# A gather by fp32 products, an earlier second layer and 17 weight slots in two expert stages

## Chip, cores and metric

One core of a Trainium2 chip runs the whole program in one launch. The metric is the device time of that launch in microseconds (us); lower is better. Engines: PE (TensorE; matmuls, and PEld its weight loads), DVE (VectorE), ACT (ScalarE), POOL (GpSimd) and SP (SyncE, which here only issues DMAs). Each engine runs its own instructions in order.

## The reference, cut to what matters

Two blocks of layers on 512 tokens of width 1024. The first has two layers, and each ends in a mixture of experts. The change touches only these two mixtures:

```python
def _ec_moe(h, router, w1, w3, w2):        # 16 experts, each takes its top 64 of 512 tokens
    probs = softmax(h @ router, over the tokens)
    gates, idx = lax.top_k(probs, cap)     # cap = 64 tokens for each expert
    xs = h[bidx, idx]                      # gather
    a = xs @ w1[e]; g = xs @ w3[e]         # 1024 x 1024 each
    y = (silu(a) * g) @ w2[e] * gates      # 1024 x 1024
    return zeros.at[bidx, idx].add(y)      # scatter

x = x + g2 * _ec_moe(modulate(rmsnorm(x)), ...)
```

All is float32.

## The kernel before

`moe` (L1079) is one expert stage; it runs twice, for layers 0 and 1. Sixteen experts go as eight pairs q = 0 to 7; the two experts of a pair share PE, each with 64 of its 128 columns (tokens).

**Weights.** The three matrices of a pair come as 24 blocks of 1 MiB: 8 of w1, 8 of w3, 8 of w2, the two experts by turns. I number the blocks of a stage from 0 to 191; pair q has 24q to 24q + 23. `expert_load` (L949) issues one block on SP's queue, into the next slot of a fixed cycle, `EORDER` (L275): -1 is one of the four buffers of the ring pool, 0 to 9 are pools of one 8 KB (per partition) buffer each, opened one above the other for this stage (`more`, L1094), -2 is a buffer of the long-lived pool. There are 15 slots, so block b goes where block b - 15 lay and its DMA waits on SP until the last matmul that reads that block is done; the loads behind it in SP's queue wait with it. The first 15 are issued ahead of the stage, while PE still runs the projection of the mixer before (`pre`, L1100), each as soon as its memory is free.

**One pair.** `expert_mm` (L1157) takes the blocks in rounds of two, 16 PE instructions a round (each fp32 matmul is two instructions). w1 and w3 go into four PSUM banks `mm`. ACT and DVE make m = silu(w1) * w3 in the tile `em`; PE transposes it (L1263), DVE or ACT copies it back, and w2 (`expert_mm` again, into two `ac` banks) follows. `weigh` (L1265) multiplies by the gates and makes two parts of the result in `ey`, and `scatter` (L1271) adds it to x by products with a one-hot; that is done in the rounds 2 and 3 of the next pair's w1 (`rest`). `em` and `ey` share one buffer.

**The gather.** The token rows of pair 0 are gathered by fp32 products of x with a scaled one-hot (`pick_first`, L1132), between the first rounds of its w1. The other pairs go in groups (1), (2, 3), (4, 5), (6, 7): `gather` (L1103) makes the one-hot `oh` on DVE from the positions `pT` that `topk` finds, `pick` (L1119) gathers by products, `gates` (L1139) gathers the gate values. The products are made in two parts: `xn` is the normalized x as a rounded fp32r part (`xnh`) and the rest (`xnl`), `prp` the same of the probabilities; so a group has 8 column blocks x 4 token tiles x 2 parts = 64 products, of 128 columns for one pair and 256 for two. ACT makes xnh and DVE xnl (L1244, L1245). The gather for the next group stands behind the last w3 of a group and ahead of that pair's transposes and w2.

**What sets the order.** On PE the order is that of the code (`manual_schedule`, L1211). On DVE, ACT and POOL a scheduler places an instruction by what is ready; on SP the loads go in the order of the code.

Of the kernel before, what the change touches and what calls it, by code (L numbers as in the profile page):

```python
# [10 lines left out]
F32 = mybir.dt.float32  # L11
F32R = mybir.dt.float32r
BF16 = mybir.dt.bfloat16
AF = mybir.ActivationFunctionType
ALU = mybir.AluOpType
AX = mybir.AxisListType
PSUM = bass.MemoryType.PSUM

P = 128
D = 1024  # L20
# [5 lines left out]
NT = 4  # L26
# [243 lines left out]
class Builder:  # L270
    NBASE = 4
    X1, X2, X3, X4, X5, X6 = 2, 1, 3, 1, 7, 1
    NSTREAM, SDEPTH, SBUFS = 3, 2, 4
    EXTRA = 10
    EORDER = ((3, 2, 8, 9, 7, 0, 1, -1, -1, -1, -1, 4, 5, 6, -2), (-1, 7, 0, 6, 1, 8, 9, -1, -1, 5, -1, 2, 3, 4, -2))  # L275

    def __init__(self, ctx, tc, a, out):
        self.ctx, self.tc, self.nc, self.a, self.out = ctx, tc, tc.nc, a, out
# [800 lines left out]
    def moe(self, l, fin):  # L1079

        nc, a, tc, x = self.nc, self.a, self.tc, self.x
# [4 lines left out]
        pos = mp.tile([16, 512], BF16, name=f"pos{l}")  # L1086
        pT = mp.tile([P, NT, 16], F32, name=f"pT{l}")
        gts = mp.tile([P, 8], F32, name=f"gts{l}")

        xn = [self.pp.tile([P, NT, D], F32R, tag="hp0", name=f"xnh{l}"), mp.tile([P, NT, D], F32R, name=f"xnl{l}")]  # L1090
        prp = mp.tile([P, NT, 8, 2, 2], F32R, name=f"prp{l}")
        rt = self.pp.tile([P, KD // 2, 512], F32, tag="hp1", name=f"rt{l}")

        more = [es.enter_context(tc.tile_pool(name=f"r2{i}{l}", bufs=1, reuse_waits="tile")) for i in range(self.EXTRA)]  # L1094
# [8 lines left out]
        def gather(qs):  # L1103

            n = len(qs)
            oh = mp.tile([P, NT, 2, P], F32R, tag="oh", name=self.nm("oh"))
            o = oh[:, :, 0:n].rearrange("p t q (e s) -> p t (q e) s", e=2)
            nc.vector.tensor_tensor(o, self.iota[:, None, None, :].to_broadcast([P, NT, 2 * n, 64]),
                                    pT[:, :, 2 * qs[0]:2 * qs[0] + 2 * n, None].to_broadcast([P, NT, 2 * n, 64]), op=ALU.is_equal)
            xs = mp.tile([P, KD, 2, P], F32, tag="xsT", name=self.nm("xsT"))  # L1110
            return xs, oh
# [7 lines left out]
        def pick(qs, xs, oh):  # L1119
            w = len(qs) * P  # L1120
            for k0 in range(0, KD, 2):
                p = self.mm("ac" if k0 % 4 else "tr")
                for k in (k0, k0 + 1):
                    pk = p[:, (k - k0) * 256:(k - k0) * 256 + w]
                    for i in range(2):
                        for t in range(NT):
                            nc.tensor.matmul(pk, xn[i][:, t, k * P:(k + 1) * P], oh[:, t, 0:len(qs)].rearrange("p q s -> p (q s)"),  # L1127
                                             start=(i == t == 0), stop=(i == 1 and t == NT - 1))
                for k in (k0, k0 + 1):
                    modulate(k, xs[:, k, 0:len(qs)].rearrange("p q s -> p (q s)"), p[:, (k - k0) * 256:(k - k0) * 256 + w])  # L1130

# [7 lines left out]
        def gates(qs, oh):  # L1139

            p = self.mm("tr")
            v = p[:, 0:4 * len(qs)].rearrange("p (q u e) -> p q u e", u=2, e=2)
            for i, q in enumerate(qs):
                for t in range(NT):
                    if q:
                        nc.tensor.matmul(p[:, 4 * i:4 * i + 4], oh[:, t, i], prp[:, t, q].rearrange("p u e -> p (u e)"),
                                         start=(t == 0), stop=(t == NT - 1))
                    else:
                        nc.tensor.matmul(p[:, 0:2], oh0[:, 1, t], pr[:, t, 0:2], start=(t == 0), stop=(t == NT - 1))
            for e in range(2):  # L1150
                s = slice(64 * e, 64 * e + 64)
                if qs[0]:
                    nc.vector.tensor_reduce(gts[s, qs[0]:qs[0] + len(qs)], v[s, :, :, e], axis=AX.X, op=ALU.add)
                else:
                    nc.vector.tensor_copy(gts[s, 0:1], p[s, e:e + 1])

        def expert_mm(ps, lhs, before=None):  # L1157
            for i in range(4):
# [52 lines left out]
        with tc.manual_schedule(engines={mybir.EngineType.PE}):  # L1211
            for q in range(8):
# [20 lines left out]
                if q == 0:  # L1233
                    p = self.mm("tr")
                    sc = mp.tile([P, 512], F32R, tag="sc", name=self.nm("sc"))
                    for t in range(NT):
                        nc.tensor.transpose(p[:, t * P:(t + 1) * P], oh0[:, 1, t], self.ident)
                    nc.scalar.activation(out=sc, in_=p, func=AF.Copy)
                    gates((0,), None)
                    g2 = self.bcast_gate(mp, l, 1)  # L1240
                    with tc.issue_after(ohi.ins):
                        topk()
                    for t in range(NT):
                        nc.scalar.activation(out=xn[0][:, t], in_=x[:, t], func=AF.Copy, scale=rr[:, t:t + 1])  # L1244
                        nc.vector.scalar_tensor_tensor(xn[1][:, t], x[:, t], rr[:, t:t + 1], xn[0][:, t].bitcast(F32), op0=ALU.mult, op1=ALU.subtract)  # L1245
                    for t in range(NT):
                        v = pr[:, t].rearrange("p (q e) -> p q e", e=2)
                        nc.scalar.activation(out=prp[:, t, :, 0], in_=v, func=AF.Copy)
                        nc.vector.tensor_tensor(prp[:, t, :, 1], v, prp[:, t, :, 0].bitcast(F32), op=ALU.subtract)
                em = self.pp.tile([P, 2, D], F32, tag="hp1", name=self.nm("em"))  # L1250
                m, mT = em[:, 0], em[:, 1].rearrange("p (k s) -> p k s", k=KD)
                for j in range(2):
                    js = slice(j * 512, (j + 1) * 512)
                    nc.scalar.activation(out=m[:, js], in_=acc[0][j], func=AF.Silu)  # L1254
                    nc.vector.tensor_tensor(m[:, js], m[:, js], acc[1][j], op=ALU.mult)  # L1255
                if q == groups[g][-1] and q < 7:
                    xs, oh = gather(groups[g + 1])
                    pick(groups[g + 1], xs, oh)
                    gates(groups[g + 1], oh)
                for j in range(2):  # L1260
                    p = self.mm("tr")
                    for k in range(4):
                        nc.tensor.transpose(p[:, k * P:(k + 1) * P], m[:, (4 * j + k) * P:(4 * j + k + 1) * P], self.ident)  # L1263
                    nc.any.tensor_copy(mT[:, 4 * j:4 * j + 4], p.rearrange("p (k s) -> p k s", k=4))
                def weigh(p, j, e):  # L1265

                    nc.vector.scalar_tensor_tensor(p, p, gts[:, q:q + 1], g2[:, j * 512:(j + 1) * 512], op0=ALU.mult, op1=ALU.mult)  # L1267
                    self.lastw = nc.scalar.activation(out=e[:, 0], in_=p, func=AF.Copy)  # L1268
                    nc.vector.tensor_tensor(e[:, 1], p, e[:, 0].bitcast(F32), op=ALU.subtract)
# [8 lines left out]
                if q < 7:  # L1278
                    py = [self.mm("ac") for _ in range(2)]
                    expert_mm(py, lambda k, s: mT[:, k, 64 * s:64 * s + 64])  # L1280
                    ey = self.pp.tile([P, 2, 2, 512], F32R, tag="hp1", name=self.nm("ey"))
                    for j in range(2):
                        weigh(py[j], j, ey[:, j])
                    left.append(lambda t, j, f=scatter, ey=ey: f(t, j, ey[:, j]))
                    continue

# [1185 lines left out]
```

## Time and profile before

| what | us |
|---|---|
| median of 3 runs | 2370.78 (2370.53 to 2378.63) |
| the profiled execution | 2370.2 |
| its span, first to last instruction | 2368.1 |
| PE busy in the span | 2183.7 (92%) |
| DVE busy | 1025.3 (43%) |
| ACT busy | 614.8 (26%) |
| POOL busy | 361.0 (15%) |

The expert stages lie at 439 to 917 and 1140 to 1619 us. A row of a timeline gives the start, the duration, engine, line, operation and what is written from what (names without numbers); xN is a count of merged instructions, and in brackets stands the idle time of the engine before the row and what ended it. A window's row gives the busy time of each engine in it with its instructions, the granted clock of PE as a share of full speed (1.00 is 2.4 GHz, 0.50 is 1.2 GHz), the busy share of the DMA engines and the GB/s that they moved.

### The profile page before, as it was taken

Reading aid. Unit: us, or ns where it says so; the run is one execution under the profiler, and the core shown is the slowest. Engines: PE = TensorE matmul, PEld = TensorE weight load, DVE = VectorE, ACT = ScalarE, POOL = GpSimd, SP = SyncE. Lnnn points to the kernel's source line nnn. Section 1 sums busy time; section 2 is a strip of 40 time slices with the busy share of each in tenths; the row PEclk is TensorE's granted clock in tenths of the full one; section 3 lists DMA queues with packets and bytes.
Section 4 is the critical chain, followed back from the end, with each engine's and each line's share of the span. In section 5 each row is a group of like instructions: output and inputs, shape, how many; then the busy total and the mean of one; then the engine's idle time right before and its main releaser. Section 6 shows DMA issues by size and latency. Waiting matters only on the chain.

```text
span 2368.1 us, 29818 instructions
## 1 busy us (share of the span) xinstructions
PE 2183.7 (92%) x11928; PEld 1319.5 (56%) x11928; DVE 1025.3 (43%) x2051; ACT 614.8 (26%) x1149; POOL 361.0 (15%) x390
## 2 busy tenths in 40 slices
PE   7997899999998987999899998987999889999998
PEld 2772487554342424667554433334766667777776
DVE  5645563622121214883522221215665666535642
ACT  3336123210000004333200000005433334333442
POOL 2221113000000002012000000002233431232232
PEclk9998799989999999999889999998999999999999
DMA  8537215679999997744789999996211220141131
GB/s 323 190 106 266 107 61 209 244 321 419 418 419 418 419 419 274 249 160 160 301 324 420 420 420 420 420 418 207 71 37 46 79 63 28 37 151 45 45 112 71
DMA packets 190196, 551.64 MB, mean 233 GB/s; under 512 B 12625, under 2 KB 69849, under 8 KB 182762
## 3 DMA queue, kind: packets, MB, share of 16 engines
q1 hardware_dynamic: 186282, 533.47, 58.4%
q0 software_dynamic: 2768, 11.71, 1.5%
q10 hardware_dynamic: 1008, 4.56, 0.5%
q8 instruction: 94, 1.54, 0.3%
q14 instruction: 44, 0.36, 0.0%
HBM read 545.51 MB, written 4.19 MB: 232 GB/s over the span
## 4 chain that ended last, share of the span: by engine, by line
PE 60%; DMA 13%; DVE 5%; POOL 3%; ACT 2%; issue 1%; POOLq 0%; DVEq 0%; ACTq 0%; SPq 0%
PE mm L1166 14%; DMA ring<-in_exp_w_dram 12%; PE ac L1166 6%; PE ac L1553 4%; PE mm L904 4%; PE ac L1554 4%; PE ac L1555 4%; PE mm L351 4%; PE mm L1662 2%; PE tr L1127 2%; PE ac L351 2%; PE ac L1127 2%; PE ac L1275 1%; PE tr L1275 1%; PE tr L1710 1%
## 5 line engine op out<-in xcount | busy, mean ns | idle before, releaser
L1166 PE MATMUL mm<-ring,xsT 128*64 128x512 f32 x2048 | 472.2, 596 | 38.1 <-DMA ring<-in_exp_w_dram 38.1
L1166 PEld LDWEIGHTS mm<-ring,xsT 128*64 128x64 f32 x2048 | 149.8, 137 | 328.1 <-issue 250.0
L1166 PE MATMUL ac<-ring,em 128*64 128x512 f32 x896 | 203.9, 601 | 13.2 <-DMA ring<-in_exp_w_dram 12.3
L1553 PE MATMUL ac<-hC,sth 128*128 128x512 f32 x504 | 211.5, 420 | 1.7 <-ACT msg L2249 1.7
L1554 PE MATMUL ac<-hC,sth 128*128 128x512 f32 x504 | 206.5, 410 | 0.0
L1555 PE MATMUL ac<-hC,stl 128*128 128x512 f32 x504 | 204.4, 406 | 0.2 <-DVE stl L334 0.2
L1166 PEld LDWEIGHTS ac<-ring,em 128*64 128x64 f32 x896 | 64.7, 138 | 142.1 <-issue 111.3
L1529 ACT ACTIVATE sth<-ring 128x512 fp32r<-128x512 f32 x126 | 79.2, 630 | 145.9 <-PE ac L1554 127.7
L1255 DVE TENSOR_TENSOR em<-em,mm 128x512 f32<-128x512 f32 x32 | 21.8, 688 | 218.9 <-PE mm L1166 216.9
L1553 PEld LDWEIGHTS ac<-hC,sth 128*128 128x128 f32 x504 | 96.6, 192 | 25.9 <-ACT msg L2249 4.0
L1267 DVE SCALAR_TENSOR_TENSOR ac<-ac,gts,gate 128x512 f32<-128x512 f32 x28 | 21.2, 759 | 204.5 <-PE ac L1166 204.5
L1555 PEld LDWEIGHTS ac<-hC,stl 128*128 128x128 f32 x504 | 96.2, 191 | 20.9 <-DVE stl L334 0.7
L1554 PEld LDWEIGHTS ac<-hC,sth 128*128 128x128 f32 x504 | 96.4, 191 | 20.1 <-issue 2.1
L1276 DVE TENSOR_TENSOR x<-ac,x 128x512 f32<-128x512 f32 x64 | 41.6, 686 | 140.8 <-PE ac L1275 140.8
L334 POOL TENSOR_TENSOR wsl<-ring,wsh 128x1024 fp32r<-128x1024 f32 x7 | 16.7, 2386 | 547.8 <-ACT wsh L340 547.8
L904 PE MATMUL mm<-pwh,cp 128*128 128x512 f32 x256 | 86.2, 416 | 4.6 <-ACT cp L1473 3.2
L334 DVE TENSOR_TENSOR stl<-ring,sth 128x512 fp32r<-128x512 f32 x84 | 63.1, 752 | 62.6 <-ACT sth L1529 60.7
L351 PE MATMUL mm<-hB,wsh 128*128 128x512 f32 x256 | 85.1, 407 | 1.5 <-ACT hB L418 0.7
L1254 ACT ACTIVATE em<-mm 128x512 f32<-128x512 f32 x32 | 18.9, 597 | 238.6 <-PE mm L1166 238.6
L334 POOL TENSOR_TENSOR stl<-ring,sth 128x512 fp32r<-128x512 f32 x42 | 54.4, 1295 | 154.7 <-ACT sth L1529 154.4
L1268 ACT ACTIVATE ey<-ac 128x512 fp32r<-128x512 f32 x28 | 16.7, 597 | 212.0 <-PE ac L1166 209.4
L351 PE MATMUL ac<-hA,wsh 128*128 128x512 f32 x224 | 71.4, 399 | 0.0
(804 smaller groups left out, 3840.4 us busy)
## 6 DMA issues: line engine op xcount, KB each, us to landing
ring<-in_exp_w_dram SPq DMA_DIRECT2D x384, 1024.0 KB, 17.8
ring<-in_w_in_dram SPq DMA_DIRECT2D x40, 1024.0 KB, 5.2
mblk<-in_w_mod_dram SPq DMA_DIRECT2D x40, 1024.0 KB, 5.0
ring<-in_cf_w_dram SPq DMA_DIRECT2D x12, 1024.0 KB, 8.0
ring<-in_w_out_dram SPq DMA_DIRECT2D x8, 1024.0 KB, 5.1
ring<-in_w_mod_dram SPq DMA_DIRECT2D x4, 1024.0 KB, 21.9
hW<-in_w_mod_dram SPq DMA_DIRECT2D x4, 1024.0 KB, 23.6
wbr<-in_w_branch_dram SPq DMA_DIRECT2D x16, 256.0 KB, 2.6
```

The lines of the kernel that those rows point to most:

```text
L334: (self.nc.gpsimd if self.nlo % self.lomod == 0 else self.nc.vector).tensor_tensor(out, a, b, op=ALU.subtract)
L351: self.nc.tensor.matmul(p[:, :n], x[:, k], y[:, k], start=(k == 0 and i == 0), stop=(stop and k == K - 1 and i == 2))
L904: nc.tensor.matmul(ps[t], u, v[:, k], start=(bias is None and s == 0 and k == 0 and i == 0), stop=(s == 3 and k == 1 and i == 2))
L1127: nc.tensor.matmul(pk, xn[i][:, t, k * P:(k + 1) * P], oh[:, t, 0:len(qs)].rearrange("p q s -> p (q s)"), start=(i == t == 0), stop=(i == ...
L1166: nc.tensor.matmul(ps[j][64 * s:64 * s + 64, :], lhs(k, s), wt[s][:, kk, j * 512:(j + 1) * 512], start=(k == 0), stop=(k == KD - 1))
L1275: nc.tensor.matmul(p, sc[:, t * P:(t + 1) * P], e[:, i], start=(i == 0), stop=(i == 1))
L1276: nc.vector.tensor_tensor(x[:, t, js], p, x[:, t, js], op=ALU.add)
L1529: nc.scalar.activation(out=hi, in_=src, func=AF.Copy)
L1553: nc.tensor.matmul(self.sps, hi[:, k], hh, start=(kk == 0), stop=False)
L1554: nc.tensor.matmul(self.sps, hi[:, k], hl, start=False, stop=False)
L1555: nc.tensor.matmul(self.sps, lo[:, k], hh, start=False, stop=(kk == KD - 1))
L1662: self.nc.tensor.matmul(p[s], lb[:, c], r, start=start, stop=stop)
```

## The change

Four edits, all in `moe` and its slots:

- The gather of the groups (1) to (6, 7) is by fp32 products of one `xn` (no parts), 32 for a group; `xnl` (16 KB per partition) and `prp` are gone, with the DVE and ACT work that made them. An fp32 product is two PE instructions.
- The gates are gathered by fp32 products with `pr`, and copied instead of summed from two parts.
- For pair 0 alone, `gather`, `pick` and `gates` of the next pair come after its w2 and `weigh`; for the other groups they stay ahead of the transposes.
- Two slots more, 10 and 11, of 8 KB: 17 in the cycle, in a new order. Blocks 0 to 16 are issued ahead of the stage, and block b waits for block b - 17.

```diff
--- before.py
+++ after.py
@@ -271,8 +271,8 @@
     NBASE = 4
     X1, X2, X3, X4, X5, X6 = 2, 1, 3, 1, 7, 1
     NSTREAM, SDEPTH, SBUFS = 3, 2, 4
-    EXTRA = 10
-    EORDER = ((3, 2, 8, 9, 7, 0, 1, -1, -1, -1, -1, 4, 5, 6, -2), (-1, 7, 0, 6, 1, 8, 9, -1, -1, 5, -1, 2, 3, 4, -2))
+    EXTRA = 12
+    EORDER = ((3, 2, 8, 9, 10, 7, 11, 0, 1, -1, -1, -1, -1, 4, 5, 6, -2), (-1, 7, 0, 6, 1, 8, 9, 10, -1, -1, 5, 11, -1, 2, 3, 4, -2))
 
     def __init__(self, ctx, tc, a, out):
         self.ctx, self.tc, self.nc, self.a, self.out = ctx, tc, tc.nc, a, out
@@ -1086,9 +1086,7 @@
         pos = mp.tile([16, 512], BF16, name=f"pos{l}")
         pT = mp.tile([P, NT, 16], F32, name=f"pT{l}")
         gts = mp.tile([P, 8], F32, name=f"gts{l}")
-
-        xn = [self.pp.tile([P, NT, D], F32R, tag="hp0", name=f"xnh{l}"), mp.tile([P, NT, D], F32R, name=f"xnl{l}")]
-        prp = mp.tile([P, NT, 8, 2, 2], F32R, name=f"prp{l}")
+        xn = self.pp.tile([P, NT, D], F32, tag="hp0", name=f"xn{l}")
         rt = self.pp.tile([P, KD // 2, 512], F32, tag="hp1", name=f"rt{l}")
 
         more = [es.enter_context(tc.tile_pool(name=f"r2{i}{l}", bufs=1, reuse_waits="tile")) for i in range(self.EXTRA)]
@@ -1103,7 +1101,7 @@
         def gather(qs):
 
             n = len(qs)
-            oh = mp.tile([P, NT, 2, P], F32R, tag="oh", name=self.nm("oh"))
+            oh = mp.tile([P, NT, 2, P], F32, tag="oh", name=self.nm("oh"))
             o = oh[:, :, 0:n].rearrange("p t q (e s) -> p t (q e) s", e=2)
             nc.vector.tensor_tensor(o, self.iota[:, None, None, :].to_broadcast([P, NT, 2 * n, 64]),
                                     pT[:, :, 2 * qs[0]:2 * qs[0] + 2 * n, None].to_broadcast([P, NT, 2 * n, 64]), op=ALU.is_equal)
@@ -1122,10 +1120,9 @@
                 p = self.mm("ac" if k0 % 4 else "tr")
                 for k in (k0, k0 + 1):
                     pk = p[:, (k - k0) * 256:(k - k0) * 256 + w]
-                    for i in range(2):
-                        for t in range(NT):
-                            nc.tensor.matmul(pk, xn[i][:, t, k * P:(k + 1) * P], oh[:, t, 0:len(qs)].rearrange("p q s -> p (q s)"),
-                                             start=(i == t == 0), stop=(i == 1 and t == NT - 1))
+                    for t in range(NT):
+                        nc.tensor.matmul(pk, xn[:, t, k * P:(k + 1) * P], oh[:, t, 0:len(qs)].rearrange("p q s -> p (q s)"),
+                                         start=(t == 0), stop=(t == NT - 1))
                 for k in (k0, k0 + 1):
                     modulate(k, xs[:, k, 0:len(qs)].rearrange("p q s -> p (q s)"), p[:, (k - k0) * 256:(k - k0) * 256 + w])
 
@@ -1139,20 +1136,13 @@
         def gates(qs, oh):
 
             p = self.mm("tr")
-            v = p[:, 0:4 * len(qs)].rearrange("p (q u e) -> p q u e", u=2, e=2)
             for i, q in enumerate(qs):
                 for t in range(NT):
-                    if q:
-                        nc.tensor.matmul(p[:, 4 * i:4 * i + 4], oh[:, t, i], prp[:, t, q].rearrange("p u e -> p (u e)"),
-                                         start=(t == 0), stop=(t == NT - 1))
-                    else:
-                        nc.tensor.matmul(p[:, 0:2], oh0[:, 1, t], pr[:, t, 0:2], start=(t == 0), stop=(t == NT - 1))
+                    nc.tensor.matmul(p[:, 2 * i:2 * i + 2], oh[:, t, i] if q else oh0[:, 1, t], pr[:, t, 2 * q:2 * q + 2],
+                                     start=(t == 0), stop=(t == NT - 1))
             for e in range(2):
                 s = slice(64 * e, 64 * e + 64)
-                if qs[0]:
-                    nc.vector.tensor_reduce(gts[s, qs[0]:qs[0] + len(qs)], v[s, :, :, e], axis=AX.X, op=ALU.add)
-                else:
-                    nc.vector.tensor_copy(gts[s, 0:1], p[s, e:e + 1])
+                nc.vector.tensor_copy(gts[s, qs[0]:qs[0] + len(qs)], p[s, e:e + 2 * len(qs):2])
 
         def expert_mm(ps, lhs, before=None):
             for i in range(4):
@@ -1241,22 +1231,22 @@
                     with tc.issue_after(ohi.ins):
                         topk()
                     for t in range(NT):
-                        nc.scalar.activation(out=xn[0][:, t], in_=x[:, t], func=AF.Copy, scale=rr[:, t:t + 1])
-                        nc.vector.scalar_tensor_tensor(xn[1][:, t], x[:, t], rr[:, t:t + 1], xn[0][:, t].bitcast(F32), op0=ALU.mult, op1=ALU.subtract)
-                    for t in range(NT):
-                        v = pr[:, t].rearrange("p (q e) -> p q e", e=2)
-                        nc.scalar.activation(out=prp[:, t, :, 0], in_=v, func=AF.Copy)
-                        nc.vector.tensor_tensor(prp[:, t, :, 1], v, prp[:, t, :, 0].bitcast(F32), op=ALU.subtract)
+                        nc.scalar.activation(out=xn[:, t], in_=x[:, t], func=AF.Copy, scale=rr[:, t:t + 1])
                 em = self.pp.tile([P, 2, D], F32, tag="hp1", name=self.nm("em"))
                 m, mT = em[:, 0], em[:, 1].rearrange("p (k s) -> p k s", k=KD)
                 for j in range(2):
                     js = slice(j * 512, (j + 1) * 512)
                     nc.scalar.activation(out=m[:, js], in_=acc[0][j], func=AF.Silu)
                     nc.vector.tensor_tensor(m[:, js], m[:, js], acc[1][j], op=ALU.mult)
-                if q == groups[g][-1] and q < 7:
+                def more():
                     xs, oh = gather(groups[g + 1])
                     pick(groups[g + 1], xs, oh)
                     gates(groups[g + 1], oh)
+                    return xs
+
+                last = q == groups[g][-1] and q < 7
+                if last and q:
+                    xs = more()
                 for j in range(2):
                     p = self.mm("tr")
                     for k in range(4):
@@ -1281,6 +1271,9 @@
                     ey = self.pp.tile([P, 2, 2, 512], F32R, tag="hp1", name=self.nm("ey"))
                     for j in range(2):
                         weigh(py[j], j, ey[:, j])
+                    if last and q == 0:
+
+                        xs = more()
                     left.append(lambda t, j, f=scatter, ey=ey: f(t, j, ey[:, j]))
                     continue
```

## Rows read from the trace of the kernel before

**Rows 1.** DMA issues of the page: count, KB each, median us to landing

```profile
ring<-in_exp_w_dram SPq DMA_DIRECT2D x384, 1024.0 KB, 17.8
```

**Rows 2.** Windows of the first stage: engines, clock, DMA share, GB/s

```profile
493.50:503.30 9.80, 9.80 (x41) 6.05 (x42) 2.55 (x5) 1.04 (x2) 0.00 (x0) 0.61 0.01 2
503.30:574.00 70.70, 70.54 (x360) 30.43 (x358) 17.02 (x27) 6.42 (x11) 0.00 (x0) 1.00 1.01 408
574.00:912.00 338.00, 308.17 (x1424) 123.27 (x1420) 66.41 (x105) 24.20 (x42) 0.00 (x0) 1.00 1.03 417
```

**Rows 3.** SP in order of time, from four windows: issues of expert blocks

```profile
477.05 0.42 SPq L318 DMA_DIRECT2D ring<-in_exp_w_dram  x1
...
503.30 0.88 SPq L318 DMA_DIRECT2D ring<-in_exp_w_dram  x2
...
559.44 0.88 SPq L318 DMA_DIRECT2D ring<-in_exp_w_dram  x2
...
1259.58 0.37 SPq L318 DMA_DIRECT2D ring<-in_exp_w_dram  x1
```

**Rows 4.** Landing of the blocks issued at 503.3, 559.4 and 1259.6

```profile
DMA to landing us min/median/max: 4.7/5.8/6.8
...
DMA to landing us min/median/max: 10.3/11.3/12.2
...
DMA to landing us min/median/max: 10.0/10.0/10.0
```

**Rows 5.** PE in order of time, around the gathers for pairs 1 and 2

```profile
481.78 1.08 PE L1127 MATMUL tr<-oh,xnh 128*128 128x128 f32 x4 [1.14 <-DVE oh L1108]
...
496.28 1.97 PE L1263 MATMUL tr<-ident,em 128*128 128x128 f32 x8
...
498.17 10.25 PE L1166 MATMUL ac<-ring,em 128*64 128x512 f32 x40
...
513.40 7.03 PE L1166 MATMUL mm<-ring,xsT 128*64 128x512 f32 x32
...
545.84 0.72 PE L1127 MATMUL tr<-oh,xnh 128*128 128x256 f32 x4
...
553.51 0.95 PE L1146 MATMUL tr<-prp,oh 128*128 128x4 f32 x8
```

**Rows 6.** DVE in order of time, from three windows of the first stage

```profile
436.98 1.28 DVE L1245 SCALAR_TENSOR_TENSOR xnl<-x,rrm,xnh 128x1024 fp32r<-128x1024 f32 x1
...
482.65 1.28 DVE L1255 TENSOR_TENSOR em<-em,mm 128x512 f32<-128x512 f32 x2 [1.01 <-ACT em L1254]
...
514.38 1.45 DVE L1269 TENSOR_TENSOR ey<-ac,ey 128x512 fp32r<-128x512 f32 x2
```

**Rows 7.** Windows around the first gather and w2: the clock (third from last)

```profile
480.70:498.10 17.40, 16.32 (x76) 16.09 (x76) 4.81 (x12) 4.20 (x7) 0.00 (x0) 0.50 0.62 255
...
501.20:513.40 12.20, 12.20 (x58) 3.91 (x56) 0.76 (x1) 0.00 (x0) 0.00 (x0) 1.00 0.74 288
```

**Rows 8.** Chain that ended last, pieces: w2 of pairs 1 and 2

```profile
555.76 13.95 PE ac L1166 x64
...
603.60 13.88 PE ac L1166 x64
```

**Rows 9.** PE in order of time: fp32 products of 128 and 256 columns

```profile
449.19 1.06 PE L1136 MATMUL ac<-oh,x 128*128 128x128 f32 x8
...
126.69 5.42 PE L847 MATMUL mm<-pt,dcs 128*128 128x256 f32 x24
```

**Rows 10.** Instructions of L1136 and L847: duration ns min/median/max, first and last start

```profile
L1136 PE MATMUL ac<-oh,x x64: 274/275/421, 440.7 to 1155.9; 128*128 128x128 f32 x64
...
L847 PE MATMUL mm<-pt,dcs x128: 379/379/483, 103.0 to 341.4; 128*128 128x256 f32 x128
```

**Rows 11.** SP in order of time, in the preload: blocks 2 and 3

```profile
374.94 1.10 SPq L318 DMA_DIRECT2D ring<-in_exp_w_dram  x2
```

**Rows 12.** Window between the preload's end and the first freed slot

```profile
436.00:449.00 13.00, 11.53 (x81) 8.36 (x78) 11.72 (x29) 1.85 (x7) 0.00 (x0) 0.86 0.00 1
```

## The prediction

> **What bounds the kernel now.** I read first the page's DMA issues [rows 1]: 384 transfers of 1 MiB, 192 in each expert stage, are the bulk of all traffic. Next, the windows of the first stage [rows 2]: DMA moves 2 GB/s from 493.5 to 503.3, 408 until 574, 417 to the stage's end. So transfers run without a pause from 503.3 on, at 1.0486 MB / 417 GB/s = 2.515 us a block, and before that lies a hole. In the last of these windows PE is busy for 308.17 of 338 us: late in the stage it waits while DMA does not. A stage therefore ends when its last block lands, plus a fixed tail, and that is the end of the last hole plus the remaining blocks times 2.515 us. A faster PE late in the stage gives nothing; what counts is how SP waits for free slots early.
>
> Then SP's issues and their landings [rows 3, 4]. Block 30 is issued at 477.05; the next, 31, only at 503.30, when the first round of pair 0's w2 has freed its slot. It lands 4.7 us later, the price of one transfer on an empty queue. In between PE runs the gather for pair 1 [rows 5]: products from 481.78, gates, transposes of em from 496.28, w2 from 498.17. At 559.44, after the first w2 round of pair 1, block 55 takes 10.3 us (in the second stage, at 1259.58, 10.0), so the queue is then 10.3 - 4.7 = 5.6 us (5.3) behind the slots. That is the moment that decides below.
>
> **The change part by part.** I sum each part up to that moment, when the first w2 round of pair 1 has freed blocks 40 and 41.
>
> *Start.* A subtract for xnl, 1.28 us, stands on DVE between rk and the first one-hot [rows 6]. Without it the first gather, and all behind it, starts up to 1.2 us earlier. PE's first products ran partly at the half clock, so part may be given back or some added; bounds 0 and 3, I take 1.0. The other subtracts and prp lie beside PE work and give nothing.
>
> *w2 of pair 0 ahead of the gather.* SiLU and product of pair 0 were hidden under the gather; now PE waits for them. em's first half is ready at 482.65 + 0.7 = 483.35 [rows 6], so the transposes start at 483.4, 1.6 us later than the gather did. From there to w2 it takes 1.9 us, as now [rows 5]. w2's first round frees its slots 503.30 - 498.17 = 5.1 us after its start: at 483.4 - 1.0 + 1.9 + 5.1 = 489.4 in place of 503.30. The DMAs that this moves are SP's alone.
>
> *The clock there.* The granted clock is half from 480.7 to 498.1 and full from 501.2 [rows 7], some 3 us into w2; the low stretch begins behind the small products that follow w3. w2 of pair 0 takes 513.40 - 498.17 = 15.2 us [rows 5] against 13.95 for that of pair 1 [rows 8]. I keep 15.2; bounds 13.95 (full at once) and 16.7 (half for twice as long as now). The Trainium skill (TensorE: Matmul & The Clock Gate, What's actually happening) says that "the default state is throttled, and activity releases the throttle"; the added wait before em is a lack of activity, and read strictly w2 could run at half. The trace agrees with its other half, that a dense w2 brings the clock back. By the strict reading the sum is that of rival (c).
>
> *The gather for pair 1.* Now 64 part products start 0.213 us apart at the half clock: with gates, 481.78 to 496.28, 14.5 us [rows 5]. As 32 fp32 products of two instructions each it is again 64. The first gather of pair 0, L1136, has that form: 8 instructions in 1.06 us [rows 9], of which the last lasts 0.275 [rows 10], so (1.06 - 0.275) / 7 = 0.112 each. It comes right after a dense w2, so at the full clock: 64 x 0.112 = 7.2, gates 8 x 0.112 = 0.9, together 8.1. Saved: 6.4.
>
> *The gather for pairs 2 and 3.* Now 64 part products of 256 columns, 545.84 to 553.51, 7.67 us [rows 5]. In fp32 it is 64 instructions of 128x256. L847 has that form: 24 in 5.42 us [rows 9], the last 0.38 [rows 10], so 0.22 each. 64 x 0.22 = 14.1: 6.4 more. The gates go from 8 instructions to 16: 8 x 0.112 = 0.9 more. One-hots and modulates stay as they are.
>
> *Sum on PE.* -1.0 + 1.6 - 6.4 + 6.4 + 0.9 = +1.5: the round ends at 560.9 in place of 559.4. PE itself gains nothing.
>
> *Two more blocks.* What is issued at this moment is then not block 55 but 57, as slots 10 and 11 stand where xnl did not need to be kept. In the preload they come 5th and 7th (8th and 12th in stage 1). Slots 8 and 9, right below them, are issued at 374.94 without a wait [rows 11], and what lay above belongs to mixers that have ended, so I expect no wait. DMA is idle from 436 to 449 (1 GB/s) [rows 12]: that hides the 5 us of two more transfers. If SP had to wait for slot 10, every later load would stand behind it: rival (e).
>
> *Is the queue caught up by then?* Block 32 has the place of today's 30, whose landing ends the traffic at 493. w2 of pair 0 frees slots for 33 to 40 from 489.4 on, two per 3.4 us, so the queue runs through to about 513. The gather frees nothing. w1 of pair 1 starts at 484.3 + 15.2 + 8.1 = 507.6, its first round ends 3.6 later, block 41 lands at 507.6 + 3.6 + 4.7 = 515.9. Today's 41 lands at 503.3 + 4.7 + 10 x 2.515 = 533.1: the queue is 17 us ahead. Then every 2.515 us, so 56 lands at 553.6. Block 57 needs the round at 560.9 and DMA is idle: a second hole, made by the longer gather. 57 lands at 560.9 + 4.7 = 565.6; today at 559.4 + 10.3 + 2 x 2.515 = 574.7. Gained: 5.6 (no queue left) + 5.0 (two blocks) - 1.5 = 9.1 us. Second stage: 5.3 + 5.0 - 1.5 = 8.8.
>
> *Later gathers.* Two more cost PE 6.4 + 0.9 = 7.3 apiece. A pair without gather takes 603.60 - 555.76 = 47.8 from w2 to w2 [rows 8]; one with it 14.1 + 1.8 = 15.9 more, 63.7. From w2 of pair 1 at 557.2, four of the first and two of the second kind bring w2 of pair 7 to 875.8. Its first block, 184, lands at 565.6 + 127 x 2.515 = 885.0. So 9.2 us of cover hide them; without that cover each would cost its 7.3. Nor do they empty the queue: at the gather of pairs 4 and 5 (651 to 668) blocks up to 104 may be in, and DMA is near 98.
>
> **Rivals.** (a) *DMA does not starve at the second gather*: then block 41 decides, 17.2 us a stage, 2370.8 - 34.4 = 2336. It would need a much shorter gather; against it, the 0.22.
> (b) *DVE's order.* If DVE makes pair 1's one-hot after weighing pair 0, which ends at 514.38 + 1.45 = 515.83 [rows 6] when w2 ends at 513.40, PE waits 2.4 + 0.7 + 0.2 = 3.3 us: 2 x 3.3 lost, 2359.5. Against it: pT is ready long before, and nothing else holds that tile.
> (c) *Slower: the clock.* If the wait for em leaves the clock at half through w2 of pair 0 and the gather behind it, w2 costs 27.9 in place of 15.2, and the gather with gates 15.3 in place of 8.1: 19.9 a stage against 9 gained, 2370.8 + 2 x 10.9 = 2393. It decides from a loss of 9 us, some 18 us of dense work at half. For it: today's gather of pair 1, 14 us of products that never saw the full clock. Against it: w2 brought it back within 3 us.
> (d) *Slower: fp32 products that do not overlap.* At the 0.379 us that one such instruction lasts [rows 10] a gather for two pairs costs 24.3, w2 of pair 7 could start only at 875.8 + 3 x 10.2 = 906, where today its first block is there at about 894: 2 x 12 lost, 2395. From 9.2 / 192 + 0.22 = 0.27 us apiece PE begins to bind. Against it: L847 in a row.
> (e) *The slots come late*: SP stands, and pair 0 waits for blocks, by an estimate from five rounds that come 1 us late each 5 us a stage: 2363.
>
> **How the numbers follow.** The profiled execution took 2370.2 (span 2368.1, 2.1 around it); the median is 2370.78. The sum, 9.1 + 8.8 = 17.9, gives 2352.3 against that execution, 2352.9 against the median. Chances: this forecast 0.68, (a) 0.06, (b) 0.13, (c) 0.05, (d) 0.04, (e) 0.04. Range: at the good ends the start gives 2.0 more and w2 1.3, 3.3 a stage, with (a)'s near side some 2345; at the bad ends start +1.0, w2 +1.5, products +0.4 and (b)'s 3.3 give 6.2 a stage, 2365. It takes in (b) and (e) and leaves out (a), (c), (d), 0.15. About 0.5%, 11.9 us, can be told from no change: faster is below 2358.9, slower above 2382.6. The forecast less its bad tail (0.06), (a) and half of (b) are faster: 0.75. The tail, the rest of (b) and (e) are the same: 0.16. (c) and (d) are slower: 0.09.
>
> **What would show it.** No long hole of DMA from 493 to 503, but one of some 9 us before 563; block 57 issued near 561 and landing in under 5 us; w1 of pair 1 starting at 507 to 508; instructions 0.112 and 0.22 us apart in the two gathers; the full clock a few us into w2 of pair 0; PE still waiting for blocks at pair 7. I am wrong if that second hole is missing or ends 3 us from there, if PE waits over 2 us for em or the one-hot beyond the sum, or if PE's late waits for blocks are gone.

## The result, and the profile after

| | before | after |
|---|---|---|
| median of 20 runs (us) | 2377.35 (2370.30 to 2382.68) | 2362.72 (2356.61 to 2369.83) |
| ratio after / before | | 0.9946, 95% interval 0.9935 to 0.9957 |
| profiled execution: time, span (us) | 2370.2, 2368.1 | 2366.5, 2364.7 |
| rk of stage 0 to landing of its last block (us) | 475.1 | 466.6 |
| the same, stage 1 (us) | 474.2 | 467.6 |

By the ratio the change is worth 12.8 us of the 2370.8 on which the prediction rests, so some 2358, where 2352.9 and a gain of 17.9 were forecast: inside the range, and with 0.54% (interval 0.43 to 0.65) at the bound of 0.5%. The ratio is the one on record; the two medians alone would give 0.9938. "Landing" is the issue on SP plus the time to landing in the DMA records; rk is the DVE instruction L1070 with which a stage's gather begins, and lengths from it leave out whatever went before. In the changed kernel the products of the gather are L1124, the gates L1141, the expert products L1156, the transposes of em L1253 and the last pair's w2 L1288.

PE in order of time in the changed kernel, first stage (start, length, line, tiles out<-in, count, in brackets the wait before it), which answers to [rows 5]:

```profile
481.27 1.94 PE L1253 MATMUL tr<-ident,em 128*128 128x128 f32 x8 [2.84 <-DVE em L1240]
483.14 16.12 PE L1156 MATMUL ac<-ring,em 128*64 128x512 f32 x64
499.19 1.05 PE L1124 MATMUL tr<-oh,xn 128*128 128x128 f32 x7
...
506.44 0.95 PE L1141 MATMUL tr<-pr,oh 128*128 128x2 f32 x8
507.32 1.08 PE L1156 MATMUL mm<-ring,xsT 128*64 128x512 f32 x4
...
539.82 3.72 PE L1124 MATMUL tr<-oh,xn 128*128 128x256 f32 x16
...
553.74 1.84 PE L1141 MATMUL tr<-pr,oh 128*128 128x2 f32 x16
...
556.75 1.51 PE L1156 MATMUL ac<-ring,em 128*64 128x512 f32 x6
```

The new order is there: w2 at 483.14, the gather of pair 1 from 499.19 to 507.32, then w1. The gather for pairs 2 and 3 takes 539.82 to 553.74, 13.9 us, where it took 7.67.

SP's issues, three windows of stage 0 and one of stage 1, which answer to [rows 3]; the first blocks are 33, 41, 57, and 57 of stage 1:

```profile
488.98 0.88 SPq L318 DMA_DIRECT2D ring<-in_exp_w_dram  x2
...
510.99 0.88 SPq L318 DMA_DIRECT2D ring<-in_exp_w_dram  x2
...
560.43 0.88 SPq L318 DMA_DIRECT2D ring<-in_exp_w_dram  x2
...
1254.86 0.88 SPq L318 DMA_DIRECT2D ring<-in_exp_w_dram  x2
```

The time from issue to landing of the last of these, blocks 57 and 58 of stage 1, which answers to [rows 4]:

```profile
DMA to landing us min/median/max: 4.9/5.9/7.0
```

Windows of the first stage (engines PE, PEld, DVE, ACT, POOL, then granted clock, DMA share, GB/s), which answer to [rows 2, 7]:

```profile
477.00:487.50 10.50, 7.01 (x26) 3.35 (x26) 2.20 (x4) 4.62 (x7) 0.00 (x0) 0.51 1.02 415
489.00:552.00 63.00, 63.00 (x322) 33.74 (x319) 14.62 (x25) 5.91 (x11) 0.00 (x0) 1.00 0.98 394
552.50:560.50 8.00, 7.95 (x49) 4.94 (x49) 2.08 (x4) 1.53 (x3) 0.00 (x0) 1.00 0.07 29
560.50:904.00 343.50, 330.55 (x1508) 136.31 (x1504) 69.55 (x110) 27.45 (x50) 0.00 (x0) 1.00 1.02 416
```

The hole at 493 is gone (394 GB/s through that stretch); a second one of 8 us ends where block 57 is issued. The clock is at half, 1.2 GHz, until 487.5, some 4 us into w2, and full behind that.

The last stretch of the last w2 of stage 0 in the chain of waits (start, length, what), before:

```profile
906.83 2.82 PE mm L1295 x12
```

The same in the changed kernel, with a stretch ahead of it:

```profile
885.00 13.46 DMA ring<-in_exp_w_dram
...
898.50 3.65 PE mm L1288 x14
```

PE still waits for blocks at pair 7, and the last stretch of w2 starts 8.3 us earlier.

### The profile page after: what moved, and what is told of

It is laid out like the page before. It is cut to its first block, busy times and chain, and to the rows that moved or that the text cites. A ratio compares the mean times of both kernels' runs of the same rounds, so it can differ in the third digit from the quotient of the medians.

```text
span 2364.7 us, 29907 instructions
## 1 busy us (share of the span) xinstructions
PE 2212.5 (94%) x11984; PEld 1342.0 (57%) x11984; DVE 1013.3 (43%) x2029; ACT 616.6 (26%) x1147; POOL 361.1 (15%) x390
## 4 chain that ended last, share of the span: by engine, by line
PE 66%; DMA 7%; DVE 4%; POOL 3%; ACT 2%; issue 1%; POOLq 0%; SPq 0%; DVEq 0%; ACTq 0%
PE mm L1156 16%; PE ac L1156 8%; DMA ring<-in_exp_w_dram 6%; PE ac L1546 5%; PE mm L904 4%; PE ac L1547 4%; PE ac L1548 4%; PE mm L351 3%; PE tr L1124 2%; PE mm L1655 2%; PE ac L1124 2%; PE ac L351 2%; PE ac L1265 1%; PE tr L1265 1%; PE tr L1703 1%
## 5 line engine op out<-in xcount | busy, mean ns | idle before, releaser
L1156 PE MATMUL mm<-ring,xsT 128*64 128x512 f32 x2048 | 460.7, 595 | 16.7 <-DMA ring<-in_exp_w_dram 16.7
L1156 PEld LDWEIGHTS mm<-ring,xsT 128*64 128x64 f32 x2048 | 144.7, 137 | 299.7 <-issue 266.3
L1156 PE MATMUL ac<-ring,em 128*64 128x512 f32 x896 | 200.7, 601 | 2.7 <-DMA ring<-in_exp_w_dram 2.5
L1156 PEld LDWEIGHTS ac<-ring,em 128*64 128x64 f32 x896 | 64.1, 139 | 129.6 <-issue 118.1
```

Of the source, the lines that this page charges most:

```text
L1156: nc.tensor.matmul(ps[j][64 * s:64 * s + 64, :], lhs(k, s), wt[s][:, kk, j * 512:(j + 1) * 512], start=(k == 0), stop=(k == KD - 1))
```

## The experiments

In the table "products" says whether the gathers behind pair 0 run as part products or as fp32 products, "order" says ahead of which gather the w2 of a pair stands ("old" is behind it), and the lengths (us, good to 0.1) are from rk to the landing of block 65 (the first behind all holes; in e4 DMA starves right ahead of it and once more behind it) and of the last block, stage 0 / stage 1, each from one profile.

| kernel | products | order | slots | ratio to before (95%) | block 65 | last block |
|---|---|---|---|---|---|---|
| before | parts | old | 15 | 1 | 157.6 / 156.6 | 475.1 / 474.2 |
| before again | parts | old | 15 | | 157.5 / 156.6 | 475.0 / 474.3 |
| e1 | parts | pair 0 | 15 | 0.9906 (0.9875 to 0.9937) | 148.9 / 149.5 | 466.4 / 467.3 |
| e7 | fp32 | old | 15 | 0.9946 (0.9930 to 0.9962) | 152.2 / 153.4 | 469.7 / 471.2 |
| e3 | fp32 | pair 0 | 15 | 0.9971 (0.9950 to 0.9993) | 154.6 / 154.3 | 472.0 / 472.0 |
| e2 | fp32 | old | 17 | 0.9930 (0.9902 to 0.9958) | 147.1 / 147.5 | 463.9 / 467.7 |
| the change | fp32 | pair 0 | 17 | 0.9946 (0.9935 to 0.9957) | 149.6 / 147.7 | 466.6 / 467.6 |
| the change again (e8) | fp32 | pair 0 | 17 | 0.9906 (0.9888 to 0.9924) | 149.7 / 147.9 | 466.5 / 468.0 |
| e4 | fp32 | pairs 0, 1 | 17 | 0.9884 (0.9853 to 0.9915) | 141.7 / 142.1 | 460.7 / 463.7 |
| e6 | fp32 | pair 1 | 17 | 0.9867 (0.9848 to 0.9887) | 144.0 / 145.3 | 460.8 / 463.9 |
| e5, single pairs | fp32 | pair 0 | 17 | 0.9870 (0.9849 to 0.9892) | 142.0 / 141.9 | 458.6 / 460.7 |
| e10, the same again | fp32 | pair 0 | 17 | 0.9876 (0.9842 to 0.9911) | 141.3 / 141.4 | 458.5 / 461.5 |
| e9, single pairs | fp32 | old | 17 | 0.9898 (0.9860 to 0.9936) | 145.3 / 145.0 | 462.0 / 463.8 |

The two measurements of the change lie outside each other's intervals, while its two profiles agree within 0.4 us in both stages. So the stage lengths carry the argument below, and the ratios only the sign and rough size.

**e1: the order alone.**

```diff
...
+                if last and q:
+                    xs = more()
...
+                    if last and q == 0:
+                        xs = more()
```

> The kernel before with one edit: w2 of pair 0 ahead of the gather for pair 1; the part products, the 15 slots and xnl stay. Theory (block issued after the first w2 round of pair 1 decides): transposes 1.6 us later, gather for pair 1 right behind a dense w2 at the full clock, 64 x 0.118 + 0.9 = 8.5 in place of 14.5, w2 of pair 0 about 0.8 longer: the round ends at 555.8 in place of 559.4, and block 55 finds an empty queue and lands at 560.5 in place of 569.7. Gain 9.2 us a stage, 18 us in all, as much as the whole change. Rival (the two more blocks and the cheaper first gather make the gain, the order only pays for the wait for em): the stage ends no earlier, 0 to 3 us later, since the buffers are the same.

The order alone shortens the stages by 8.7 and 6.9 us, as much as the whole change. PE in order of time at pair 1's gather and what stands around it:

```profile
489.67 15.18 PE L1166 MATMUL ac<-ring,em 128*64 128x512 f32 x64
504.77 0.66 PE L1127 MATMUL tr<-oh,xnh 128*128 128x128 f32 x4
505.27 0.61 PE L1127 MATMUL tr<-oh,xnl 128*128 128x128 f32 x4
...
511.97 0.56 PE L1146 MATMUL tr<-prp,oh 128*128 128x4 f32 x4
512.45 2.79 PE L1166 MATMUL mm<-ring,xsT 128*64 128x512 f32 x12
```

The issue of blocks 55 and 56 on SP:

```profile
558.58 0.88 SPq L318 DMA_DIRECT2D ring<-in_exp_w_dram  x2
```

Their time to landing:

```profile
DMA to landing us min/median/max: 5.1/6.1/7.1
```

At the full clock the part products need 504.77 to 511.97, 7.2 us or 0.112 each, no more than fp32 products. Block 55 is issued 558.58 - 440.86 = 117.7 us after rk, where it was 559.44 - 436.90 = 122.5, and finds the queue empty.

**e7: the fp32 products alone**, and **e3: both, without the two slots.** e7 is the kernel of e2 (below) with the slots of before, e3 the changed kernel with them:

```diff
-    EXTRA = 12
+    EXTRA = 10
...
```

> The kernel before with the fp32 products alone: 15 slots, w2 behind the gather for pair 0 as before. Theory (the fp32 products of the first gather bring the clock back themselves, which saves some 5 us there, and about 2 us more in w2 of pair 0; the longer second gather takes 7 back, but the 5 us by which the queue stood behind the slots absorb most of it): block 57 lands 5 us earlier after rk than before (132.6 against 137.8), about 8 to 11 us faster than before in all, ratio 0.9955 to 0.9965. Rival (the terms of the prediction: without the new order the gather of pair 1 stays at the half clock, 15.3 us, and the gather for pairs 2 and 3 is 7.3 us longer): block 55 would land 1.5 us later than before, ratio 1.001.

> The changed kernel with one edit: 15 slots in the old order; fp32 products and the new order of w2 and gather stay. Theory: the first w2 round of pair 1 ends at 560.4 as in the changed kernel, what is issued then is block 55, which lands at 565.1 against 569.7: 4.6 us a stage, 9 us in all faster than the kernel before; 5 us a stage less than the changed kernel. Rival (the order alone does it, the slots add nothing): the same stage ends as the changed kernel, 903.5 in the first stage.

PE of e7 in order of time around pair 1's gather, in the old place ahead of w2:

```profile
480.52 3.75 PE L1124 MATMUL tr<-oh,xn 128*128 128x128 f32 x16 [1.14 <-DVE oh L1106]
...
488.20 1.95 PE L1124 MATMUL ac<-oh,xn 128*128 128x128 f32 x16
...
492.11 13.95 PE L1156 MATMUL ac<-ring,em 128*64 128x512 f32 x64
505.89 5.32 PE L1156 MATMUL mm<-ring,xsT 128*64 128x512 f32 x24
```

Two windows of e7 with the granted clock there:

```profile
478.50:485.20 6.70, 5.28 (x26) 5.20 (x27) 2.61 (x5) 3.47 (x6) 0.00 (x0) 0.50 1.02 421
485.30:505.00 19.70, 19.65 (x120) 10.68 (x120) 3.31 (x7) 2.54 (x5) 0.00 (x0) 1.00 0.67 257
```

The issue of blocks 55 and 56 in e7:

```profile
558.95 0.88 SPq L318 DMA_DIRECT2D ring<-in_exp_w_dram  x2
```

The same issue in e3; in both kernels block 55 lands 4.8 us after it:

```profile
561.06 0.88 SPq L318 DMA_DIRECT2D ring<-in_exp_w_dram  x2
```

In the old place, where the part products stayed at half through all 14.5 us [rows 5, 7], the fp32 products run at half only until 485.2: products 9.5 us (480.52 to 489.99), and w2 13.95 throughout at the full clock. w1 of pair 1 starts 505.89 - 437.94 = 68.0 us after rk, where it was 513.40 - 436.90 = 76.5. The rival of e7, a gather that stays at half, is out. The two edits do not add: the order gives 8.7 and 6.9 us, the fp32 products 5.4 and 3.0, both together 3.1 and 2.2. Each pays for the same thing, pair 1's gather at the full clock; together it is paid once, while the wait for em and the longer second gather are both owed. In e3 block 55 is issued 561.06 - 437.64 = 123.4 us after rk, later than in either alone (117.7 and 121.0). It lands 4.6 us earlier than before (128.2 for 132.8), as e3's expectation had it; 1.5 us of that are gone by block 59, which lands late.

**e2: the change with pair 0 in the old order.**

```diff
-                if last and q:
+                if last:
...
-                    if last and q == 0:
+                    if False:
```

> The changed kernel with one edit: the gather for pair 1 back ahead of w2 of pair 0; fp32 products and 17 slots stay. Theory: the gather for pair 1 runs at the half clock, 72 x 0.213 = 15.3; with the start 1.0 earlier and 7.3 more in the gather for pairs 2 and 3 the first w2 round of pair 1 ends at 566.5, block 57 lands at 571.2 against 574.7 before: 3.5 us a stage, 7 us in all faster than the kernel before. Rival (the two blocks bring 5 us a stage by themselves, whatever PE does): 10 us in all or more.

PE of e2 in order of time, in the same stretch as that of e7 above:

```profile
482.29 3.75 PE L1124 MATMUL tr<-oh,xn 128*128 128x128 f32 x16 [1.14 <-DVE oh L1106]
...
493.60 13.95 PE L1156 MATMUL ac<-ring,em 128*64 128x512 f32 x64
507.39 4.03 PE L1156 MATMUL mm<-ring,xsT 128*64 128x512 f32 x18
```

The 7 us that theory gave were missed (the ratio gives 16.6). The rows say why: theory had the gather at the half clock, and the clock came back inside it. Stage 0 is 2.7 us shorter than in the change, stage 1 the same. w1 of pair 1 starts 507.39 - 439.64 = 67.8 us after rk, and 507.32 - 436.99 = 70.3 in the change. So with fp32 products the new order costs PE 2.5 us in stage 0; in stage 1, where w1 of pair 1 starts 69.7 us after rk in both, it costs nothing, and the stage ends alike. It fills the first hole, but the second decides. From e3 to the change the two slots alone give 5.4 and 4.4 us, close to the 5.0 of the prediction.

**e4: w2 ahead of the gather for pair 1 too, and e6: for pair 1 only.** The diff is that of e4; in e6 the two conditions are q != 1 and q == 1.

```diff
-                if last and q:
+                if last and q > 1:
...
-                    if last and q == 0:
+                    if last and q < 2:
```

> The changed kernel with one edit: for pair 1, too, w2 comes ahead of the gather (for pairs 2 and 3). Theory: the hole of DMA ahead of block 57 (issue at 560.4 because of the 15.4 us gather) vanishes; w2 of pair 1 starts 1.5 us after w3's end, at 541.4, ends at 555.4, the gather stands behind it, the first w1 round of pair 2 ends at 574.4 and block 65 lands at 579.1, against 594.8 in the kernel before: 15.7 us a stage, unless PE becomes the bound at pair 7, where it would be ready only 3 us ahead of the blocks; 13 to 15.7 a stage, 26 to 31 us in all. Rival (that hole is not what ends the stage; PE or another wait takes its place): within 3 us of the changed kernel, 8 us a stage.

> The changed kernel with the order of pair 0 as before (gather of pair 1 ahead of its w2) and the new order for pair 1 instead (its w2 ahead of the gather for pairs 2 and 3). Theory: with fp32 products the new order at pair 0 costs about 2.5 us (w1 of pair 1 started 67.8 us after rk with the old order, 70.3 with the new), and with no second hole the landing of block 41, freed by the first round of w1 of pair 1, decides: block 57 lands near 117.7 us after rk, against 120.3 with both pairs' w2 first. So 2.5 us a stage better than that kernel (27.5 us faster than before): about 32 us faster than before, ratio 0.9865 (0.984 to 0.989). Rival (the hole of 6 us before block 33, open again with the old order, puts the queue so far behind that block 41 is not yet waited for): as good as or worse than with both pairs' w2 first, ratio 0.9885 or more, with block 57 landing 120 us or later after rk.

PE of e4 in order of time at w2 of pair 1:

```profile
543.90 13.95 PE L1156 MATMUL ac<-ring,em 128*64 128x512 f32 x64
557.78 3.72 PE L1124 MATMUL tr<-oh,xn 128*128 128x256 f32 x16
```

The issue of blocks 57 and 58 in e4:

```profile
547.57 0.88 SPq L318 DMA_DIRECT2D ring<-in_exp_w_dram  x2
```

Two windows of e4, columns as above:

```profile
552.50:560.50 8.00, 8.00 (x39) 3.99 (x36) 2.82 (x4) 1.20 (x2) 0.00 (x0) 1.00 1.02 420
575.00:620.00 45.00, 44.70 (x206) 16.21 (x204) 7.45 (x13) 2.37 (x4) 0.00 (x0) 1.00 0.97 390
```

The issue of blocks 33 and 34 in e6:

```profile
495.57 0.88 SPq L318 DMA_DIRECT2D ring<-in_exp_w_dram  x2
```

Two windows of e6:

```profile
489.00:502.50 13.50, 13.46 (x75) 6.05 (x75) 1.95 (x4) 1.72 (x4) 0.00 (x0) 1.00 0.49 188
502.50:575.00 72.50, 72.20 (x342) 34.16 (x340) 16.43 (x26) 7.01 (x12) 0.00 (x0) 1.00 1.03 418
```

e4 shows that the second gather made the second hole: with w2 ahead of it, block 57 is issued 107.4 us after rk in place of 123.4, DMA moves 420 GB/s where it moved 29, and block 64 lands 9.2 us earlier (137.9 after rk for 147.1). Of these 9.2 (stage 0), 3.3 are lost again at block 65 and behind it (390 GB/s from 575 to 620): now the gather for pairs 2 and 3 stands behind w2 and frees no slot. e6's ratio is the 0.9865 expected, but its trace says the rival: the first hole is open again (188 GB/s), block 65 lands 2.2 and 3.2 us later than in e4, and the stages end when e4's do (460.8 and 463.9 us after rk), not 2.5 us earlier. A ratio that agrees is no proof of the mechanism.

**e5: a gather for every pair, e10: once more, and e9: with pair 0 in the old order.**

```diff
-        left, groups = [], ((0,), (1,), (2, 3), (4, 5), (6, 7))
+        left, groups = [], tuple((q,) for q in range(8))
...
-                g = q if q < 2 else q // 2 + 1
+                g = q
```

> The changed kernel, but every gather is for one pair (eight gathers of 64 instructions of 128 columns in place of five); only pair 0's w2 stays ahead of the gather behind it. Theory (the hole before block 57 is the length of the second gather): the gather for pair 2 is 64 x 0.112 = 7.2 us and 8 gates 0.9 in place of 14.1 and 1.8, so w2 of pair 1 starts near 550 in place of 556.75, block 57 is issued near 553.7 and lands near 558.4, where the queue behind block 41 alone would bring it at 556. A hole of about 2 us is left in place of 8, so some 6 us a stage: 12 us faster than the change, about 25 us faster than the kernel before, ratio 0.989 (0.987 to 0.992). Rival (more, smaller gathers expose more waits for one-hots and modulates on PE, and PE becomes the bound late in the stage): no better than the change, ratio 0.994 or more, with PE no longer waiting for blocks at pair 7.

> The kernel with single-pair gathers once more, beside the one with the old order. The stages take 458.6 and 460.7 us after rk again, within 1 us; what lies behind stage 1 follows the half clock there (765.5 us with 64.6 us of it the first time; 757 if it is some 45 us). Ratio 0.985 to 0.989.

> The kernel with single-pair gathers, but with pair 0's w2 behind the gather of pair 1 as before. What is asked is whether the new order is worth anything once the second hole is gone. Theory: the first hole, 6 us before block 33, is open again, and what the queue loses there is not given back, as no later hole hides it: block 57 lands near 124 us after rk (as in the kernel with the new order at pair 1 alone) in place of 120 to 121, each stage ends 3 us later than with single pairs and the new order (461.6 and 463.7 us after rk against 458.6 and 460.7), ratio 0.9895 against 0.987. Rival (the 2.5 us by which w1 of pair 1 starts earlier in the old order make up for the hole): the same as single pairs with the new order within 1 us a stage, ratio 0.987.

PE of e5 in order of time at the gather of pair 2:

```profile
541.49 2.05 PE L1124 MATMUL tr<-oh,xn 128*128 128x128 f32 x16
...
548.74 0.95 PE L1141 MATMUL tr<-pr,oh 128*128 128x2 f32 x8
549.55 1.28 PE L1253 MATMUL tr<-ident,em 128*128 128x128 f32 x8
550.86 5.37 PE L1156 MATMUL ac<-ring,em 128*64 128x512 f32 x24
```

The issue of blocks 57 and 58 in e5:

```profile
554.54 0.88 SPq L318 DMA_DIRECT2D ring<-in_exp_w_dram  x2
```

A window of e5 across what was the second hole:

```profile
551.00:560.50 9.50, 9.50 (x46) 3.22 (x47) 0.56 (x1) 0.00 (x0) 0.00 (x0) 1.00 0.92 358
```

The gather that decides takes 7.2 us in place of 13.9, block 57 is issued 8 us earlier after rk, and of the hole 9.5 x (1 - 358 / 417) = 1.3 us are left. The stages are 8.0 and 6.9 us shorter than in the change; e10 repeats them within 0.9. By the ratios, 29 to 31 us faster than before, the intervals do not set it apart from e4, e6 and e9; by the stages, the shortest of all by 2 us and more, it is the best version measured. No run has the part products with single-pair gathers or with w2 first at pair 1, so whether they would do as well there stays open. In e9, with the first hole open again, the stages are 3.4 and 3.1 us longer than in e5, as expected: once the second hole is gone, the new order is worth its place.

**e8 and e11: the change and the kernel before once more.**

> The changed kernel once more, for a second profile of it. What is asked is where the 5 us went that the forecast had too much. If they belong to the kernel, the mixer between the stages again takes 2.6 us longer than in the profile of before (228.5 against 225.9 us from the last block of stage 0 to rk of stage 1) and the part behind stage 1 again 9 us longer (765.0 against 756.0). If they are a matter of where the clock happens to dip, both parts differ from the first profile by as much, and follow the time at the half clock (40.3 us in the mixer and 64.7 us behind stage 1 in the first profile, 29.1 and 37.4 us in before). The ratio is 0.9946 either way, 0.993 to 0.997.

> The kernel before once more, for a second profile. If the part behind stage 1 (756.0 us in the first profile, 757.6 to 767.1 in those of the other kernels) and the mixer between the stages (225.9; 225.1 to 230.6) follow the clock and not the edits, this profile lies in the same band, with the stages within 1 us of 475.1 and 474.2 us after rk. If they belong to the edits, it gives 756 and 225.9 again.

A window near the end of the program, columns as above, in the first profile of the change:

```profile
2129.00:2142.00 13.00, 13.00 (x57) 10.26 (x56) 3.89 (x16) 2.73 (x6) 1.28 (x1) 0.51 0.00 1
```

One at the same place in the second profile of before:

```profile
2132.00:2149.00 17.00, 17.00 (x94) 13.09 (x92) 2.05 (x9) 1.69 (x4) 1.28 (x1) 0.50 0.00 1
```

And in the first profile of before:

```profile
2129.00:2149.00 20.00, 20.00 (x165) 16.01 (x164) 7.38 (x30) 4.40 (x11) 1.67 (x2) 1.00 0.06 21
```

From the last block of stage 1 to the end the change took 765.0 us, of which 64.7 at the half clock, and again 757.7 with 47.1; before took 756.0 with 37.4, and again 761.9 with 50.2. Over all thirteen profiles this part lies between 756.0 and 767.1 and grows by 0.36 us for each us at the half clock. The 9 us that the first two profiles show there is thus not the change's: the dip comes and goes in either kernel. The mixer between the stages took 225.9 in both profiles of before, 228.5 and 227.9 in those of the change, but 225.1 in e5 and e7, which have the fp32 products too, and 227.3 in e10, the same program as e5. So the fp32 products alone do not explain it; whether something in the change costs 2 us there stays open.

## Why the prediction was right, and where it was not

Step by step, as the prediction put it:

- **Start**, -1.0 (0 to 3): w3 and the small products were done 41.4 us after rk (481.27 less the wait of 2.84, less 436.99) in place of 43.7 (481.78 - 1.14 - 436.90) [rows 5]: -2.3, inside the bounds.
- **Wait for em**, +1.6: 2.84 in place of 1.14, +1.7.
- **w2 of pair 0**, 15.2: 16.05 (483.14 to 499.19), as the clock came back some 4 us into it and not 3. Rival (c) is out: the clock was full from 487.5, long before the gather. The Trainium skill (TensorE: Matmul & The Clock Gate, What's actually happening) says that activity releases the throttle; the trace agrees, with 2.4 GHz back some 4 us into a dense w2, and bears out nothing of the stricter reading that the prediction set beside it.
- **Gather of pair 1 with gates**, 8.1: 8.13. **Gather for pairs 2 and 3**, 14.1: 13.92; gates 1.7 for 1.8. Rival (d) is out.
- **Sum and queue**: block 57 at 560.43 for 560.9, in part by luck, as the start came out 1.3 us better and w2 0.85 us worse; in stage 1 it lands 4.9 us after its issue, for 4.7. The gain, forecast at 9.1 and 8.8: block 59 of stage 0 lands 133.2 us after rk in place of 142.7, 9.5 earlier, block 57 of stage 1 at 127.8 in place of 136.7, 8.9. The second hole, 8.0 us for some 9, rules out rival (a). w1 of pair 1 at 507.32 for 507.6: no wait for the one-hot, rival (b) is out. Blocks 4 and 6 on slots 10 and 11 were issued without a wait; rival (e) is out.

**The term that was too large** is the step from the deciding moment to the time. The stages are 8.5 and 6.6 us shorter, 15.1, not 17.9. The prediction let every block behind the deciding one land 2.515 us after the one ahead, and some do not. In stage 0 blocks 61 and 150 land 1.3 and 1.2 us later than their turn, where before one did (129, 1.5): 9.5 less 1.0 is the 8.5. In stage 1 blocks 67, 155 and 183 land 1.5, 1.5 and 1.0 us late, where before one block did (125, 1.4; block 190 is late in both); the second profile of the change shows the same but for small shifts (61 and 149; 67, 155 and 183). At 183 lie five small loads of POOL for the next phase, the first of them before (POOL in order of time):

```profile
1608.99 0.62 POOL L1496 DMA_DIRECT2D k_minclT<-in_k_minclT_dram  x1 [447.33 <-DMA ring<-in_exp_w_dram]
```

And in the changed kernel:

```profile
1570.90 0.62 POOL L1489 DMA_DIRECT2D k_minclT<-in_k_minclT_dram  x1 [419.31 <-DMA ring<-in_exp_w_dram]
```

They have moved from the last 3 us of the stage (471.2 after rk) to 438.9 after rk, which the prediction did not look for. That they delay block 183 is inferred from the place. At blocks 61, 67 and 155 the DMA records have one load of instructions each (16 KB on queue 8, at 573.9, 1283.7 and 1504.1, about 1 us long), 2.5 to 2.7 us ahead of the landing, and there one of the 16 pieces in which a block lands comes 1.2 to 1.6 us behind the other 15. That these loads are the cause is inferred as well: no run moves them. The rest, 15.1 against a ratio worth 12.8 in one measurement and 22 in the other, lies in the parts between and behind the stages, where the clock's dips move by as much as is sought.

**The attribution that was wrong.** The prediction gave the 6.4 us saved in pair 1's gather to fp32 products behind a dense w2. The clock is what saves it, and either edit alone brings that: parts behind w2 take 7.2 (e1), fp32 products in the old place 9.5 (e7). What the prediction did not ask is what the part products cost at the full clock. Had it, it would have seen that fp32 products behind w2 give nothing there and cost 7 us at the second gather, so that with the new order their one use is the room for two slots: e1, with neither, has the same stages (466.4, 467.3) as the change (466.6, 467.6).

## What to carry to other kernels

Price each part of a change with the other parts in place as well as alone: two edits that cure the same stall do not add, and their costs do. Where transfers set the end, find the last moment at which they starve; what counts is the work of PE right ahead of the slots freed there, so split or move that work (single-pair gathers, w2 first) before making anything else faster. Compare lengths within a stage from a fixed instruction, when the clock in other parts of the program moves the total by as much as the change does.

## What was not expected of the hardware

- In the same place, 64 part products (fp32r, 128 columns, 0.213 us apart) never saw the full clock in 14.5 us [rows 5, 7], while 32 fp32 products of the same tiles had it back 4.7 us after they began (480.52 to 485.2, e7). At the full clock both forms run at 0.112 us an instruction. Why one brings the clock back and the other does not, no run here shows.
- The parts cost as much as fp32 products at 128 columns (7.2 us for the products of a pair, e1 and the change), but at 256 columns 7.67 [rows 5] against 13.9: what fp32 products cost beside parts depends on the width.
- Time behind the stages varies by 11 us between the thirteen profiles with where the clock dips, 0.36 us for each us at half.
- Blocks in a full stream land late where instructions are loaded. From block 66 to 182 the thirteen profiles have 30 blocks that land over 0.9 us later than their turn; 29 of them have a 16 KB load of instructions 2.1 to 4.3 us ahead of the landing, and in these 29 one of the block's 16 pieces lands 1.0 to 1.7 us behind the rest. Most of the 275 such loads there delay no block.
